# A transformer pair on one Trainium2 core: the second block's scores with the queries' lower parts in a tile of 128 rows, half of them zero

## The chip, the cores and the metric

The kernel runs on one core of one Trainium2 chip. A core has TensorE (matrix products into PSUM), VectorE, ScalarE and GpSimd (elementwise work), SyncE (issues transfers) and 16 DMA engines. The metric is device time in microseconds for one execution, the median of several.

## The reference

One sequence of 256 tokens with 2048 channels passes a first block (a mixer, memory attention, a gated feed-forward) and then a second block of two layers, which works on these tokens and on 256 context tokens. The change concerns the second block's attention. Each of its eight heads has two half heads of 64 channels, and the difference of two softmaxes is applied to the values:

```python
def _diff_attn(qb, k_all, v_all, lam):
    s = jnp.einsum('bqhid,bkhid->bhiqk', qb.astype(jnp.float32) * ATTN_SCALE, k_all.astype(jnp.float32))
    p = jax.nn.softmax(s, axis=-1)
    a = p[:, :, 0] - lam * p[:, :, 1]
    return jnp.einsum('bhqk,bkhe->bqhe', a.astype(v_all.dtype), v_all)
```

In the first layer both the tokens' and the context's queries attend (the tokens to 512 keys, the context to its own 256). In the second layer only the tokens' queries do.

## The kernel before

**Products.** An operand of 32 bits is split into an upper part of reduced precision (type fp32r) and a lower part that holds the rest, and a product is three products: upper x upper, upper x lower, lower x upper. Weights stream from memory through four buffers (raw) in pieces of 128 x 1024; ScalarE writes the upper part (whi), VectorE the lower (wlo), each into four buffers, up to three pieces ahead of TensorE (split_ahead, LK = 3). The method group runs the products of one group of weight blocks, some 96 to 192 of them, into a pair of PSUM banks (acc).

**Background work.** Everything else stands in lanes of Python generators. While group writes out the weight products, it calls tick four times per piece, and tick takes a step from each lane whose operands are ready by a planner's estimate of the engines' clocks (class Meter, costs per operation). So the order on each engine is fixed when the program is built. TensorE, VectorE, ScalarE and GpSimd each run their queue in that order.

**The scores.** qk_gen (lane q) takes the projected queries or keys of one head out of PSUM, rotates them and builds stacked tiles. For a half head i, rows 64i to 64i+63 hold its own channels. For keys, the tile st[i] has the upper part in these rows and the lower part in the other 64. For queries, st[i] has the upper part in both halves, so that one product of 128 rows gives upper x upper plus upper x lower. The queries' lower parts of both half heads lie in one tile, lo, each in its 64 rows. scores (called by attn2, lane B) then adds lower x upper with a second product, of 64 rows, into the same bank:

```python
                mm(S[i], q[i][:, o:o + P], k[i], start=True, stop=False)
                mm(S[i], ql[w, o:o + P], k[i][w], start=False, stop=True)
```

For the tokens' queries (u = 0, 1) these products have 512 columns, four per call. For the context's queries (u = 2, first layer only) they have 256 columns, eight per call. softmax2 follows on VectorE and ScalarE, attn2_t transposes the result on TensorE, and tail (lane b2) multiplies by the values and takes the head's norm, for which two small operations run on GpSimd (rstd). PSUM has four banks for all background work (aux).

**Tiles.** In the first layer the tiles st and lo come from the common heap of 60 tiles of 128 x 512 (s.qkp = s.heap in second). In the second layer they have a pool of their own, qkp, with 10 tiles (line 771).

**Lines.** Every operation goes through the planner's helper at line 342, so the trace tells operations apart by their tiles. bk is a background bank; the products of the scores show as bk<-st,st and bk<-st,lo.

Of the kernel before, what the change touches and what calls it, by code (L numbers as in the profile page):

```python
# [16 lines left out]
P = 128  # L17
# [25 lines left out]
# ---------------------------------------------------------------- the order of the weights  # L43
# [171 lines left out]
def lay(inp):  # L215
    """Layout only: every array is a reordering or a concatenation of inputs."""
# [51 lines left out]
# ---------------------------------------------------------------- when the engines get to their work  # L268
class Meter:
    """Passes instructions on and keeps an estimate of the time at which each engine is done with them, by which  # L270
    the background work is placed between the large products."""
# [24 lines left out]
    def table(s, args):  # L296
        """what it costs to get another table of functions"""
        n = next((s.TABLES[x] for x in args if isinstance(x, AF) and x in s.TABLES), s.tab)
        s.tab, old = n, s.tab
        return 0.0 if n == old else 1.28  # L300
# [45 lines left out]
# ---------------------------------------------------------------- the program  # L346
class Acc(tuple):
    """Two banks as one row of 1024"""
# [7 lines left out]
class Kern:  # L356
# [7 lines left out]
    # ---- memory  # L364
# [30 lines left out]
    # ---- background work  # L395
# [3 lines left out]
    def step(s, lane):  # L399
        """One step; a step yields the number of aux banks that it leaves in use (1 if nothing is said)"""  # L400
        q = s.lanes.get(lane)
        while q:
            s.meter.last = 0.0
            try:
                n = next(q[0])
                s.held[lane] = 1 if n is None else n
                s.ready[lane] = s.meter.last + LAG
                return True
            except StopIteration:
                q.popleft()  # L410
                s.held[lane] = 0
        return False
# [4 lines left out]
    def tick(s):  # L417
        """Steps of the background work whose operands are there by now"""
        m = s.meter.clk
        for ln in sorted(s.lanes):  # L420
            if ln != "w" and s.lanes[ln] and s.ready.get(ln, 0.0) <= m["P"] and s.fits(ln):
                s.step(ln)
        if s.lanes.get("w") and not s.quiet and m["V"] <= m["P"] + WLAG:
            s.step("w")
# [4 lines left out]
    def pump(s, lanes=None):  # L429
        """A step of the lane that is ready first; true if any did something"""  # L430
        for ln in sorted(lanes or s.lanes, key=lambda ln: (s.ready.get(ln, 0.0), ln)):
            if (lanes or ln != "w") and s.lanes[ln] and s.fits(ln) and s.step(ln) and s.meter.last:
                return True
        return False
# [8 lines left out]
    def finish_lane(s, ln, alone=False):  # L443
        """alone: the lane needs neither others nor banks"""
        s.force = alone
        while alone and s.lanes.get(ln):
            s.step(ln)
        s.force = False
        s.until(lambda: not s.lanes.get(ln))
# [4 lines left out]
    # ---- the stream of weights  # L454
# [9 lines left out]
    def split_hi(s, j):  # L464
        """The upper part of piece j"""
        q, o, w = s.subs[j]
        hi = s.hip.tile([P, MH], F32R, name=s.nm("whi"), tag="whi")
        s.nc.scalar.copy(hi[:, :w], s.raws[q][:, o:o + w])
        s.hl[j] = [hi, None]
        s.nhi = j + 1  # L470

    def split_lo(s, j):
        """What the upper part leaves"""
        q, o, w = s.subs[j]
        hi = s.hl[j][0]
        lo = s.hl[j][1] = s.lop.tile([P, MH], F32R, name=s.nm("wlo"), tag="wlo")
        s.nc.vector.tensor_sub(lo[:, :w], s.raws[q][:, o:o + w], hi[:, :w].bitcast(F32))
        s.nlo = j + 1

    def split_ahead(s, pos):  # L480
        """The parts of the pieces that come next, as far as they are there"""
        end = min(s.cur - 1 + LK, len(s.subs) - 1)
        if pos in HPOS and s.nhi <= end:
            q = s.subs[s.nhi][0]
            while s.nload < min(len(PIECES), q + EK):
                s.load_next()
            if s.there(s.raws[q]):
                s.split_hi(s.nhi)
        if pos in LPOS and s.nlo <= end and s.nlo < s.nhi:
            s.split_lo(s.nlo)  # L490
# [13 lines left out]
    def group(s, name, *segs, quiet=False, half=None):  # L504
        """The products of one group of weight blocks; segs: per 256 tokens, k -> (hi, lo). With half, the first half of
        the tokens gets ahead with the last pieces, and half(acc) is called when it is done."""
# [55 lines left out]
    # ---- small pieces  # L562
# [8 lines left out]
    def rowsum(s, parts, n):  # L571
        """[P, n] partial sums (AP) -> [P, 1]"""
        r = s.sm("rs")
        s.nc.vector.tensor_reduce(r[:, 0:1], parts, AX.X, ALU.add)
        return r[:, 0:1]

    def turned(s, get, gain, dst, ks):
        """dst[k] (hi, lo) = (x^T) * gain(k); get(t, k): [P tokens, P]"""
# [20 lines left out]
    def rb_tile(s, R, b=None):  # L599
        """R [P tokens, 2] -> [P, 256], every row the tokens' factors"""  # L600
        b = b or s.accum()
        for t in range(2):
            s.nc.tensor.matmul(b[:, t * P:t * P + P], R[:, t:t + 1].to_broadcast([P, P]), s.ident, start=True, stop=True)
        r = s.rbp.tile([P, T], F32, name=s.nm("Rb"), tag="rb")
        s.nc.scalar.copy(r, b[:, 0:T])
        return r
# [18 lines left out]
    def stats(s, x, R, xT=None):  # L625
        """the sums of squares of x[t][c] -> rstd [P, 2]; where xT is given, after it"""
# [10 lines left out]
    def stats_of(s, name, R, n=2, start=lambda: True, eng=None):  # L637
        """the same for an input"""
# [12 lines left out]
    def ahead(s, src, n=2, eng=None):  # L651
        """parts of an input, each loaded ahead of its use"""
# [8 lines left out]
    def laid(s, name):  # L661
        """an input that is laid out by columns"""
        return s.ahead([s.ap[name][i] for i in range(8)])

    def busy(s):
        """whether the DMA engines have got much to do"""
        return not s.force and s.meter.dma > s.meter.clk["P"] + DGAP

    def later(s, d):
        """nothing for d us"""  # L670
# [5 lines left out]
    def scaled(s, parts, gain, dst, gap=0.0):  # L676
        """dst[k] (hi, lo) = part k * gain(k)"""
# [18 lines left out]
    def out_chunk(s, acc, row, yg, ss, c):  # L696
        """acc [P, 2 x 512] -> yg[t] = acc * row, the sums of squares of acc into ss"""
# [8 lines left out]
    def residual(s, yg, ss, x, xn, xT, chunk, wait=True):  # L706
        """xn = x + rmsnorm(y), and what chunk(c) does with a chunk of it to get to xT"""
# [40 lines left out]
    def program(s):  # L748
# [22 lines left out]
        with s.tc.tile_pool(name="qkp", bufs=10) as s.qkp:  # L771
            s.layer(1)

    # ---------------------------------------------------------------- first block
# [110 lines left out]
    def inputs(s):  # L885
        """what the background work needs"""
# [42 lines left out]
    def shift(s, a, b):  # L929
        """z = a * R; z + (prev - z) * mu"""  # L930
# [28 lines left out]
    def rwkv(s, p):  # L959
        """Two heads; h's own rows are 64h.., its other rows hold the other side of sums over 128."""  # L960
# [124 lines left out]
        # the chunks in order  # L1085
# [212 lines left out]
    # ---------------------------------------------------------------- memory attention and the feed-forward  # L1298
    def memory_ffn(s):
# [16 lines left out]
        def normed(yg, ss, x, g, tap):  # L1316
            """x + rmsnorm(y), the next norm's transposed operand and rstd, as background work"""
# [125 lines left out]
    def ffn_up(s, acc, j, hid, Rb):  # L1443
        """blocks: gate j, value j, gate j+1, value j+1"""
# [27 lines left out]
    # ---------------------------------------------------------------- second block  # L1472
    def modulation(s, l, n0, n1):
        """columns n0..n1 (of 128) of silu(c) @ w_mod + b_mod, for c and c_ctx"""
# [64 lines left out]
        if n0 == 0:  # L1539
            # lambda  # L1540
# [10 lines left out]
    def affine(s, get, g, dst, ks):  # L1551
        """dst[k] (hi, lo) = x^T * G + B, two tiles of tokens"""
# [119 lines left out]
    def y_split(s, l):  # L1672
        """the parts of the mixed output, as they come, for the product with w_out"""
# [18 lines left out]
    def rope_half(s, a, o):  # L1692
        """a (PSUM) [P, 256] -> o rotated"""
# [8 lines left out]
    def qk_gen(s, a, parts, done, q):  # L1702
        """Rotates what is x's of a (PSUM), takes it apart, and stacks the parts of each half head: the queries' upper
        parts twice, the keys' upper and lower parts."""
# [9 lines left out]
        st, lo = [s.qkt("st"), s.qkt("st")], s.qkt("lo") if q else None  # L1714
        for i in range(2):
            A.copy(st[i][w[i]], f[w[i]])
# [3 lines left out]
            d = lo[w[i]] if q else st[i][w[1 - i]]  # L1720
# [7 lines left out]
    def attn2(s, l):  # L1728
        """the scores' softmax, head by head; attn2_t turns it"""
# [41 lines left out]
    def scores(s, l, h, u):  # L1771
# [3 lines left out]
        for i in range(2):  # L1775
            w = slice(64 * i, 64 * i + 64)
            if u < 2:
                o = qo + (T if l == 0 else 0) + u * P
                mm(S[i], q[i][:, o:o + P], k[i], start=True, stop=False)
                mm(S[i], ql[w, o:o + P], k[i][w], start=False, stop=True)  # L1780
            else:
                for t in range(2):
                    b = S[i][:, t * T:(t + 1) * T]
                    mm(b, q[i][:, t * P:(t + 1) * P], k[i][:, 0:T], start=True, stop=False)
                    mm(b, ql[w, t * P:(t + 1) * P], k[i][w, 0:T], start=False, stop=True)
# [40 lines left out]
    def tail(s, l, h, ax, ac):  # L1826
        """a head's output, its norm, transposed"""
# [32 lines left out]
    def y_tile(s, l, k):  # L1860
        """the place of part k of the mixed output"""
# [137 lines left out]
    def ln_stats(s, st, n, w):  # L1999
        """per tile of tokens: scale, bias of the normalization"""  # L2000
# [13 lines left out]
    def out1_rows(s):  # L2014
        """what the last normalization is added to"""
# [44 lines left out]
    def final(s, r, st, lg, lb, t, eng):  # L2060
        """the last normalization of a tile of tokens"""
# [27 lines left out]
```

## Time and profile before

| | us |
|---|---|
| median of 3 runs | 2938.47 (2937.62 to 2941.56) |
| span of the profiled execution | 2937.8 |
| TensorE busy in it | 2890.1 (98%) |
| VectorE busy | 2074.8 (71%) |
| ScalarE busy | 1275.3 (43%) |
| GpSimd busy | 162.4 (6%) |

The span runs from the first to the last instruction of one profiled execution. A row of a timeline or of a group names the engine, the operation, the tiles it writes and reads (out<-in), the shape, and how often. For a product, 64*128 means 64 rows by 128 columns of weights, and 64x512 the moving operand. PEld is the weight load of a product. The end of a product is modelled and products overlap, so the distance between starts tells more than a duration.

### The profile page before, as it was taken

How to read it: one execution, taken by the hardware profiler on the slowest of the kernel's cores; microseconds unless marked ns; L12 is line 12 of the kernel's file. 1: busy time of each engine (PE TensorE's matmuls, PEld its weight loads, DVE VectorE, ACT ScalarE, POOL GpSimd, SP SyncE). 2: the span in 40 equal slices, each digit the busy share in tenths (PEclk: the TensorE clock that was granted, in tenths of full speed). 3: DMA queues.
4: the chain of work that ended last, by engine and by line, in shares of the span. 5: the costliest groups of instructions: out<-in, count | busy, mean ns of one | idle time of the engine just before them, and what ended most of it. 6: DMA issues, size and time to landing. Idle time of an engine off the chain costs nothing.

```text
span 2937.8 us, 53904 instructions
## 1 busy us (share of the span) xinstructions
PE 2890.1 (98%) x22059; PEld 2692.7 (92%) x22059; DVE 2074.8 (71%) x3377; ACT 1275.3 (43%) x2110; POOL 162.4 (6%) x321
## 2 busy tenths in 40 slices
PE   8899999999999999999999999999999999999997
PEld 8788887898999899998899999999999989999996
DVE  5756755687988997988768877786344563766576
ACT  5323325555444445446443554212231463555443
POOL 1001112000000000000100000000010000000001
PEclk9899999999999999999999999999999999999998
DMA  8422335765777886777764334565243453325663
GB/s 266 135 95 92 127 95 195 274 236 172 243 237 240 306 289 225 236 250 267 256 228 166 108 115 140 202 233 195 99 133 113 160 184 101 101 87 174 200 225 134
DMA packets 150857, 538.78 MB, mean 183 GB/s; under 512 B 18240, under 2 KB 18460, under 8 KB 150608
## 3 DMA queue, kind: packets, MB, share of 16 engines
q1 hardware_dynamic: 137808, 494.92, 49.4%
q0 software_dynamic: 12656, 40.37, 4.9%
q8 instruction: 173, 2.83, 0.4%
q14 instruction: 76, 0.62, 0.1%
q10 hardware_dynamic: 144, 0.03, 0.0%
HBM read 528.66 MB, written 6.59 MB: 182 GB/s over the span
## 4 chain that ended last, share of the span: by engine, by line
PE 96%; DVE 2%; DMA 1%; ACT 1%; issue 0%; POOL 0%; SPq 0%; DVEq 0%; ACTq 0%; POOLq 0%
PE acc L342 85%; PE bk L342 11%; DMA raw<-in_w_w_in 1%; DVE wlo L342 1%; ACT whi L342 0%; DVE res L342 0%; DVE junk L342 0%; DVE y L342 0%; DVE zrk L342 0%; ACT junk L342 0%; DVE yg L342 0%; POOL pw L342 0%; POOL R L342 0%; DVE ug L342 0%; DVE zr L342 0%
## 5 line engine op out<-in xcount | busy, mean ns | idle before, releaser
L342 PE MATMUL acc<-xT,whi 128*128 128x256 f32 x8992 | 1585.3, 286 | 13.0 <-ACT whi L342 12.1
L342 PEld LDWEIGHTS acc<-xT,whi 128*128 128x128 f32 x8992 | 1344.0, 193 | 27.9 <-ACT whi L342 13.0
L342 ACT CAST whi<-raw 128x1024 fp32r<-128x1024 f32 x738 | 771.4, 1050 | 906.4 <-PE acc L342 682.8
L342 PE MATMUL acc<-xT,wlo 128*128 128x256 f32 x4496 | 1130.3, 284 | 1.4 <-DVE wlo L342 1.4
L342 DVE TENSOR_TENSOR wlo<-raw,whi 128x1024 fp32r<-128x1024 f32 x738 | 896.2, 1220 | 275.5 <-ACT whi L342 273.5
L342 PEld LDWEIGHTS acc<-xT,wlo 128*128 128x128 f32 x4496 | 801.9, 193 | 2.2 <-DVE wlo L342 2.2
L342 DVE SCALAR_TENSOR_TENSOR junk<-wm,silu 128x1024 bf16<-128x1024 f32 x352 | 421.5, 1218 | 6.0 <-DMA wm<-in_w_mod 5.5
L342 PE MATMUL acc<-whi,xT 128*128 128x256 f32 (+1 forms) x1152 | 285.7, 332 | 0.9 <-ACT xT L342 0.9
L342 PE MATMUL acc<-whi,yh 128*128 128x256 f32 (+1 forms) x768 | 224.5, 319 | 0.0
L342 PEld LDWEIGHTS acc<-whi,xT 128*128 128x128 f32 x1152 | 195.9, 191 | 21.3 <-issue 2.0
L342 PE MATMUL acc<-wlo,yh 128*128 128x256 f32 (+1 forms) x640 | 194.7, 304 | 0.0
L342 PE MATMUL acc<-wlo,xT 128*128 128x256 f32 (+1 forms) x576 | 187.4, 325 | 0.0
L342 PEld LDWEIGHTS acc<-whi,yh 128*128 128x128 f32 x768 | 146.3, 191 | 9.9
L342 PE MATMUL acc<-whi,yl 128*128 128x256 f32 x512 | 144.9, 283 | 0.0
L342 PE MATMUL acc<-wlo,hh 128*128 128x512 f32 x352 | 137.3, 390 | 0.8 <-DVE wlo L342 0.8
L342 PE MATMUL acc<-whi,hh 128*128 128x512 f32 x352 | 137.2, 390 | 0.0
L342 PE MATMUL acc<-whi,hl 128*128 128x512 f32 x352 | 137.0, 389 | 0.0
L342 PEld LDWEIGHTS acc<-wlo,yh 128*128 128x128 f32 x640 | 122.3, 191 | 5.0
L342 PEld LDWEIGHTS acc<-wlo,xT 128*128 128x128 f32 x576 | 110.2, 191 | 7.0
L342 PEld LDWEIGHTS acc<-whi,yl 128*128 128x128 f32 x512 | 98.2, 192 | 0.0
L342 DVE TENSOR_REDUCE s<-bk 128x1 f32<-128x512 f32 (+1 forms) x80 | 54.2, 688 | 45.7 <-PE bk L342 45.6
L342 PE MATMUL acc<-whi,oT 128*128 128x512 f32 x256 | 80.5, 392 | 0.6 <-DVE oT L342 0.6
(346 smaller groups left out, 2668.0 us busy)
## 6 DMA issues: line engine op xcount, KB each, us to landing
raw<-in_w_w_in SPq DMA_DIRECT2D x334, 512.0 KB, 3.6
wm<-in_w_mod SPq DMA_DIRECT2D x192, 512.0 KB, 5.0
raw<-in_w_up SPq DMA_DIRECT2D x176, 512.0 KB, 4.1
raw<-in_w_w_out SPq DMA_DIRECT2D x108, 512.0 KB, 4.5
raw<-in_w_down SPq DMA_DIRECT2D x88, 512.0 KB, 4.5
raw<-in_w_wkv SPq DMA_DIRECT2D x16, 512.0 KB, 5.2
silu<-cond POOLq DMA_DIRECT2D x12, 512.0 KB, 7.6
raw<-in_w_wq SPq DMA_DIRECT2D x8, 512.0 KB, 3.5
```

Of the source, the lines that this page charges most:

```text
L342: return f(*a, **k)
```

## The change

Each half head's queries' lower part gets a tile of its own with 128 rows. Its 64 rows hold the lower part, the other 64 are set to zero by a memset on GpSimd. The second product of each pair then takes all 128 rows of this tile and of the keys' tile; the keys' lower parts in the other rows meet zeros. One more tile per head is needed, and the second layer's pool grows from 10 to 11. Apart from this the diff only removes comments.

```diff
@@ program
-        with s.tc.tile_pool(name="qkp", bufs=10) as s.qkp:
+        with s.tc.tile_pool(name="qkp", bufs=11) as s.qkp:
             s.layer(1)
...
@@ qk_gen
         w = [slice(0, 64), slice(64, 128)]
-        st, lo = [s.qkt("st"), s.qkt("st")], s.qkt("lo") if q else None
+        st, lo = [s.qkt("st"), s.qkt("st")], [s.qkt("lo"), s.qkt("lo")] if q else None
         for i in range(2):
+            if q:
+                s.nc.gpsimd.memset(lo[i][w[1 - i]].bitcast(F32), 0.0)
             A.copy(st[i][w[i]], f[w[i]])
             if q:
                 A.copy(st[i][w[1 - i]], f[w[i]])
             yield 0
-            d = lo[w[i]] if q else st[i][w[1 - i]]
+            d = lo[i][w[i]] if q else st[i][w[1 - i]]
             V.tensor_sub(d, f[w[i]], st[i][w[i]].bitcast(F32))
             yield 0
...
@@ scores
         for i in range(2):
-            w = slice(64 * i, 64 * i + 64)
             if u < 2:
                 o = qo + (T if l == 0 else 0) + u * P
                 mm(S[i], q[i][:, o:o + P], k[i], start=True, stop=False)
-                mm(S[i], ql[w, o:o + P], k[i][w], start=False, stop=True)
+                mm(S[i], ql[i][:, o:o + P], k[i], start=False, stop=True)
             else:
                 for t in range(2):
                     b = S[i][:, t * T:(t + 1) * T]
                     mm(b, q[i][:, t * P:(t + 1) * P], k[i][:, 0:T], start=True, stop=False)
-                    mm(b, ql[w, t * P:(t + 1) * P], k[i][w, 0:T], start=False, stop=True)
+                    mm(b, ql[i][:, t * P:(t + 1) * P], k[i][:, 0:T], start=False, stop=True)
```

## Rows read from the trace of the kernel before

**Rows 1.** From the page: busy time per engine, and the chain's shares by engine.
```profile
PE 2890.1 (98%) x22059; PEld 2692.7 (92%) x22059; DVE 2074.8 (71%) x3377; ACT 1275.3 (43%) x2110; POOL 162.4 (6%) x321
...
PE 96%; DVE 2%; DMA 1%; ACT 1%; issue 0%; POOL 0%; SPq 0%; DVEq 0%; ACTq 0%; POOLq 0%
```

**Rows 2.** Windows around the scores of the two layers: busy us per engine.
```profile
core 0: us, PE busy (x) PEld busy (x) DVE busy (x) ACT busy (x) POOL busy (x), PEclk, DMA share, GB/s
1580.00:1850.00 270.00, 270.00 (x2019) 246.21 (x2018) 208.23 (x410) 132.55 (x339) 9.93 (x16) 1.00 0.35 121
2498.00:2670.00 172.00, 172.00 (x1293) 156.36 (x1292) 120.72 (x237) 93.48 (x206) 6.23 (x14) 1.00 0.29 95
```

**Rows 3.** Tile st, whole span: durations, first and last start, forms; busy slices.
```profile
L342 PE MATMUL bk<-st,lo x96: 379/492/502, 1581.9 to 2664.1; 64*128 64x512 f32 x64, 64*128 64x256 f32 x32
...
busy tenths in 40 slices 0000000000000000000003453000000000431000
```

**Rows 4.** Timeline of TensorE, from 1580.83: start, duration, operation, tiles, shape, count.
```profile
1580.83 0.64 PE L342 MATMUL acc<-xT,whi 128*128 128x256 f32 x4
1581.31 0.40 PE L342 MATMUL acc<-xT,wlo 128*128 128x256 f32 x2
1581.55 0.39 PE L342 MATMUL bk<-st,st 128*128 128x512 f32 x1
1581.87 0.49 PE L342 MATMUL bk<-st,lo 64*128 64x512 f32 x1
1582.29 0.50 PE L342 MATMUL bk<-st,st 128*128 128x512 f32 x1
1582.72 0.50 PE L342 MATMUL bk<-st,lo 64*128 64x512 f32 x1
1583.15 0.74 PE L342 MATMUL acc<-xT,whi 128*128 128x256 f32 x4
1583.73 0.40 PE L342 MATMUL acc<-xT,wlo 128*128 128x256 f32 x2
```

**Rows 5.** Timeline of TensorE, from 1590.45.
```profile
1590.45 0.39 PE L342 MATMUL bk<-st,st 128*128 128x512 f32 x1
...
1592.06 0.66 PE L342 MATMUL bk<-cons,p 128*128 128x128 f32 x4
1592.47 0.72 PE L342 MATMUL acc<-xT,whi 128*128 128x256 f32 x4
```

**Rows 6.** Timeline of TensorE, from 1599.74.
```profile
1599.74 0.28 PE L342 MATMUL bk<-st,st 128*128 128x256 f32 x1
...
1602.14 0.66 PE L342 MATMUL bk<-cons,p 128*128 128x128 f32 x4
1602.55 0.48 PE L342 MATMUL acc<-xT,whi 128*128 128x256 f32 x2
```

**Rows 7.** Timeline of TensorE in the first block's feed-forward, from 960.28.
```profile
960.28 0.39 PE L342 MATMUL acc<-whi,hh 128*128 128x512 f32 x1
...
963.00 0.39 PE L342 MATMUL acc<-whi,hh 128*128 128x512 f32 x1
```

**Rows 8.** Groups by shape, window 1580 to 1850: busy us, mean ns, idle before.
```profile
L342 PEld LDWEIGHTS acc<-xT,whi 128*128 128x128 f32 x1064 | 146.1, 191 | 1.7 <-issue 1.7
...
L342 DVE TENSOR_TENSOR wlo<-raw,whi 128x1024 fp32r<-128x1024 f32 x33 | 40.2, 1218 | 0.1
L342 ACT CAST whi<-raw 128x1024 fp32r<-128x1024 f32 x33 | 34.8, 1056 | 1.9 <-PE acc L342 1.6
```

**Rows 9.** Groups of GpSimd, whole span.
```profile
L342 POOL TENSOR_TENSOR res<-res,lb 128x512 f32<-128x512 f32 x5 | 7.9, 1594 | 4.1 <-DVE res L342 4.1
...
L342 POOL MEMSET sv<- 64x64 f32 x12 | 1.8, 146 | 0.0
...
L342 POOL TENSOR_SCALAR pw<-tl 128x4 f32<-128x4 f32 x8 | 1.6, 194 | 331.7 <-ACT sq L342 331.7
```

## The prediction

> **What bounds the kernel now.** I read the chain that ended last first. It is 96% TensorE [rows 1], and TensorE is busy for 98% of the span [rows 1]. Then I read the stretches in which the change acts. The scores' products lie between 1581.9 and 2664.1 us, in two groups, one for each layer [rows 3]. In a window around each group, TensorE is busy for every microsecond (270.00 of 270.00 and 172.00 of 172.00) at a granted clock of 1.00, which is the higher level, 2.4 GHz. VectorE has 208.23 of 270 us and 120.72 of 172 us, ScalarE about half, GpSimd next to nothing, the DMA engines a third [rows 2]. So in both stretches nothing but TensorE's own stream sets the pace, and what leaves that stream should leave the total.
>
> Busy is not the same as moving, though: a product's row runs from its start to a modelled end, and a slow handover counts as busy. The pace is read from starts. In the timeline the weight products start 0.12 us apart (four from 1580.83 to 1581.31) [rows 4]; products of 128 rows and 512 columns start 0.227 us apart where they follow one another (12 steps from 960.28 to 963.00) [rows 7]. The scores' products don't. Each product of 128 rows (st, st) is followed by one of 64 rows (st, lo), and the starts go 1581.55, 1581.87, 1582.29, 1582.72, 1583.15: four products of 512 columns in 1.60 us [rows 4] where 0.91 would do. With 256 columns it is eight in 2.40 us (1599.74 to 1602.14) [rows 6] where 0.96 would do. Every handover between 128 and 64 rows costs 0.1 to 0.2 us on top of the product.
>
> **The change, part by part.** *The lower parts' products get 128 rows.* There are 96 of them, 64 with 512 columns and 32 with 256 [rows 3]. They stand in 32 blocks of four products (two per head in the first layer, 16, and two per head in the second, 16) and 8 blocks of eight (one per head in the first layer). No operation is removed: the number of products and their columns stay, the rows they read double, and the handovers between shapes go.
>
> A block of four ahead of weight products: 1.60 us, and the next four weight products take until 1583.73, 0.58 us where four others took 0.48 [rows 4]; together 2.18. Afterwards 4 x 0.227 + 0.48 = 1.39. Saved: 0.79. The timeline has ten such blocks.
>
> A block of four ahead of other 128-row products, transposes in nearly all cases: 1590.45 to 1592.06 is 1.61, and the four transposes take 0.41 until 1592.47 [rows 5]. Their first interval too must hold some of the late handover; I take 0.05 of it, half of what the block above shows, so 2.02 becomes 0.91 + 0.36 = 1.27. Saved: 0.75 (0.70 if nothing is in it, 0.80 if 0.10). There are 22.
>
> A block of eight: 2.40 and 0.41 until 1602.55 [rows 6]; afterwards 8 x 0.12 + 0.36 = 1.32. Saved: 1.49. There are 8.
>
> Sum: 10 x 0.79 + 22 x 0.75 + 8 x 1.49 = 7.9 + 16.5 + 11.9 = 36.3 us, 24.2 of them in the first layer and 12.1 in the second.
>
> The trace of before does not have this product, lo with 128 rows behind st with 128 rows. Its bounds are 0.227 us (the plain 128-row stream [rows 7]) and the 0.32 to 0.43 that stands there now. I take 0.227: the new product has exactly the shape of its neighbours, different operands don't slow the stream of rows 7, where three kinds alternate, and two products into one bank in a row are what every weight group does.
>
> Here a rule of the Trainium skill speaks against the change. The rows first: a weight load of 128x128 lasts 191 ns [rows 8], longer than the 120 ns between starts [rows 4], so loads run beside the product before them although both use all rows. The page "TensorE: Matmul & The Clock Gate", section "Part 3: Packing small matmuls — row/col tiling", says that a weight load overlaps a product under way only when the row group differs. By that rule a 128-row lo would have to load alone, a block of four would take 4 x (0.227 + 0.191) = 1.67 us against 1.60, and nothing would be saved. The trace contradicts it in the plain stream, so it is kept as a rival with a small chance (below).
>
> *24 more zero fills on GpSimd* (two per call of qk_gen with queries: 16 in the first layer, 8 in the second), each 64 rows x 512 columns. The trace has no such fill. From below: a fill of 64x64 took 0.146 us; from above: an addition of 128x512 there took 1.594 us [rows 9]. I take some 0.5 us, nearer to the fill. GpSimd is busy for 9.93 of 270 us [rows 2], so none of it is on TensorE's path. Who waits: the subtraction that writes lo, on VectorE, and behind it in VectorE's queue the splits of the weights (wlo). The cover is the lead of these splits. One is made every 270 / 33 = 8.2 us [rows 8], and the program makes them up to three pieces ahead, so even two pieces are 16 us. If the cover were gone, 24 x 0.5 to 24 x 1.6 = 12 to 38 us would come back. I cost it at nothing.
>
> *One more tile per head.* The second layer's pool grows from 10 to 11 with it. In the first layer these tiles come from the common heap of 60, which doesn't grow. Counting tiles in the order in which the program issues, I find at most 59 in use there; with one more for each of the two heads then in flight it is 61. So once or twice an engine will wait for a tile that is about to be let go. Bounds: nothing, or a few microseconds on ScalarE, VectorE or GpSimd, under the same cover. I cost it at nothing.
>
> VectorE's work is unchanged, in less time: 208 of 246 us in the first layer, 85% where it was 77%. What is late next is still TensorE.
>
> Against the profiled execution's span: 2937.8 - 36.3 = 2901.5 us. The median of the runs shown, 2938.47, is 0.67 us above that span; with it 2902.2, so 2902.
>
> **Rivals.** *Part of the gain is given back by VectorE.* Its spare time in the first layer would be 246 - 208 = 38 us. Waits for 16 fills at 1.6 us eat 26 of it and cost nothing. If each fill also waited for its tile, 3.2 us in all, 51 us would be eaten, 13.6 too many: 2916. For it: a full heap. Against it: the lead of the splits, and fills are issued on an idle engine ahead of what needs them.
>
> *The change doesn't do what it says*: the slow handover comes from something other than the number of rows (the operands' tiles, the bank), or the weight load can't be hidden as in the rule above. Then blocks keep 1.60 to 1.67 us, and the time is 2938 to 2941, say 2940. Against it: no pair of 128-row products in the rows shows such an interval.
>
> *Slower than before.* A fill waits on GpSimd for a free tile of the heap, and behind it in GpSimd's queue stand the two operations of a head's norm that wait for ScalarE (pw<-tl, eight in the first layer, 331.7 us of GpSimd's waiting in all [rows 9]). Until these are done the tail keeps its bank, and the next scores wait for a bank on TensorE, which is in order. TensorE has not waited at all in these stretches so far. It decides from 36.3 / 8 = 4.5 us per head on; at 6 us per head for eight heads 48 us come back, 2950.
>
> **How the numbers follow.** Forecast 0.79, at 2902, its own range 2897 to 2908 (the bounds of the transposes' share, 1.1 us either way; steps of 0.227 give or take 0.01 for 128 products, 1.3 us; the runs shown lie from 0.85 below to 3.1 above their median). VectorE gives back 0.12, at 2916. No effect 0.06, at 2940. Slower 0.03, at 2950. The range 2897 to 2916 leaves out the last two and the worse half of the second. A measurement of this kernel can tell about 0.2%, 6 us, from no change: faster by more 0.91, within it 0.06, slower 0.03.
>
> **What would show it.** In the profile of the changed kernel the 96 lo products stand with 128 rows; starts in a block are 0.227 and 0.120 us apart; blocks of four take 0.91 and of eight 0.96 us; the second layer's scores begin some 24 us earlier; TensorE still has no idle time in both windows. I am wrong if the starts stay over 0.3 us apart (the row count was not the cause), if TensorE shows waits for VectorE's splits or for p, or if GpSimd's fills show waits longer than a few microseconds with a tail's norm behind them.

## The result, and the profile after

The changed kernel took 2910.18 us (median of 4 runs, 2907.45 to 2915.15); the kernel before, with it, 2939.85 (4 runs). The ratio is 0.9891, 95% interval 0.9872 to 0.9909. The profiled execution has a span of 2911.2 us, 26.6 less than before. So it is faster, by 29.7 us where the sum was 36.3. The time is inside the stated range of 2897 to 2916, but outside the forecast's own, 2897 to 2908.

The blocks of scores are where to look first. The timeline of TensorE from 1590.46, a block of four ahead of weight products, answers [rows 4]:

```profile
1590.46 0.40 PE L342 MATMUL acc<-xT,wlo 128*128 128x256 f32 x2
1590.70 0.40 PE L342 MATMUL bk<-st,st 128*128 128x512 f32 x1
1590.93 0.40 PE L342 MATMUL bk<-st,lo 128*128 128x512 f32 x1
1591.17 0.39 PE L342 MATMUL bk<-st,st 128*128 128x512 f32 x1
1591.40 0.40 PE L342 MATMUL bk<-st,lo 128*128 128x512 f32 x1
1591.63 0.63 PE L342 MATMUL acc<-xT,whi 128*128 128x256 f32 x4
1592.10 0.40 PE L342 MATMUL acc<-xT,wlo 128*128 128x256 f32 x2
```

Four products now take 0.93 us (1590.70 to 1591.63) where they took 1.60, and the weight products behind them 0.47 instead of 0.58. A block ahead of transposes, from 1598.81, answers [rows 5]:

```profile
1598.81 0.40 PE L342 MATMUL bk<-st,st 128*128 128x512 f32 x1
...
1599.74 0.60 PE L342 MATMUL bk<-cons,p 128*128 128x128 f32 x4
1600.10 0.72 PE L342 MATMUL acc<-xT,whi 128*128 128x256 f32 x4
```

0.93 and 0.36 us, where it was 1.61 and 0.41. And a block of eight, from 1607.37, answers [rows 6]:

```profile
1607.37 0.28 PE L342 MATMUL bk<-st,st 128*128 128x256 f32 x1
1607.49 0.28 PE L342 MATMUL bk<-st,lo 128*128 128x256 f32 x1
...
1608.33 0.60 PE L342 MATMUL bk<-cons,p 128*128 128x128 f32 x4
1608.68 0.72 PE L342 MATMUL acc<-xT,whi 128*128 128x256 f32 x4
```

0.96 us instead of 2.40, at 0.12 per product. The tile view of lo answers [rows 3]; the 96 products have 128 rows:

```profile
L342 PE MATMUL bk<-st,lo x96: 283/394/398, 1590.9 to 2637.7; 128*128 128x512 f32 x64, 128*128 128x256 f32 x32
```

The same view for GpSimd alone has the new fills: their durations, what ended GpSimd's idle time ahead of them (us, times), and who waited for them (nothing stands below that line). POOL is GpSimd, DVE VectorE, ACT ScalarE, PE TensorE:

```profile
L342 POOL MEMSET lo<- x24: 518/521/529, 1542.1 to 2569.1; 64x512 f32 x24
...
  DVE junk L342: 80.8, 4
  PE bk L342: 66.9, 3
  DVE st L342: 20.9, 1
who waited for it (us, times):
```

Eight fills waited, 168.6 us in all and up to 38 us each, where the prediction had an engine waiting once or twice for a few microseconds. All eight belong to the first layer, whose tiles come from the heap; in the second layer, with 11 tiles, none waited. So I take it that they waited for a tile of the full heap. The last list is empty: nobody waited for a fill. But in four cases a head's norm stood right behind a fill that had waited, which was one of the stated signs of being wrong. GpSimd's timeline:

```profile
1651.18 0.52 POOL L342 MEMSET lo<- 64x512 f32 x1 [23.68 <-PE bk L342]
1658.93 0.19 POOL L342 TENSOR_SCALAR pw<-tl 128x4 f32<-128x4 f32 x1 [7.23 <-ACT sq L342]
...
1683.10 0.52 POOL L342 MEMSET lo<- 64x512 f32 x1 [22.41 <-PE bk L342]
1689.18 0.27 POOL L342 TENSOR_SCALAR pw<-tl 128x4 f32<-128x4 f32 x1 [5.55 <-ACT sq L342]
```

After such a fill the norm's operation still waited 5.55 to 7.80 us for ScalarE, so the fill did not delay it. The windows around the scores answer [rows 2] (columns as there):

```profile
1580.00:1830.00 250.00, 250.00 (x2051) 246.82 (x2050) 210.39 (x415) 133.59 (x338) 17.33 (x30) 1.00 0.42 138
2474.00:2640.00 166.00, 166.00 (x1342) 162.60 (x1341) 121.01 (x240) 95.17 (x209) 8.33 (x18) 1.00 0.32 102
```

TensorE is still busy throughout; VectorE is at 84% and 73% where it was at 77% and 70%. So every gain should have arrived, and a comparison of starts shows where it went. From the first score of the first layer to the first of the second it was 2498.61 - 1581.55 = 917.06 us and is 2483.87 - 1590.70 = 893.17: 23.9 us gained. From there to the end it was 439.19 and is 427.33: 11.9 gained. Together 35.8. In absolute time the second layer's scores begin only 14.7 us earlier, where some 24 had been stated, because the first score comes later, at 1590.70 instead of 1581.55: 9.15 us were lost ahead of the first product that the change touches. On TensorE the instructions up to there are the same, in the same order, in both kernels.

The loss lies between 200 and 460 us, among the first block's small products: product by product, the changed kernel is 0.2 us ahead at 188 us and 9.9 behind at 463. Windows of the kernel before and then of the changed one; the last three numbers are TensorE's granted clock, the DMA share and GB/s:

```profile
200.00:260.00 60.00, 60.00 (x453) 52.11 (x453) 30.65 (x73) 18.48 (x41) 5.86 (x11) 0.91 0.24 80
350.00:380.00 30.00, 30.00 (x391) 26.42 (x389) 16.24 (x33) 5.25 (x12) 7.30 (x15) 1.00 0.34 102
430.00:460.00 30.00, 30.00 (x195) 25.02 (x194) 12.69 (x32) 8.62 (x24) 6.80 (x12) 0.89 0.24 79
```

```profile
200.00:260.00 60.00, 60.00 (x422) 50.71 (x419) 27.56 (x67) 17.04 (x40) 3.66 (x8) 0.83 0.22 71
350.00:380.00 30.00, 30.00 (x303) 26.87 (x301) 15.01 (x26) 6.67 (x16) 2.81 (x9) 0.83 0.30 88
430.00:460.00 30.00, 30.00 (x214) 25.43 (x213) 11.65 (x28) 8.22 (x21) 1.23 (x2) 0.83 0.22 71
```

The mean clock of 0.83 means that a third of such a stretch ran at the lower level, 1.2 GHz; before it was 0.89 to 1.00. Whether this is chance or belongs to the changed program is what the first runs ask.

### The profile page after: what moved, and what is told of

It reads as the page before. It is cut to its first block, busy times and chain, and to the rows that moved or that the text cites. A ratio compares the mean times of both kernels' runs of the same rounds, so it can differ in the third digit from the quotient of the medians.

```text
span 2911.2 us, 53963 instructions
## 1 busy us (share of the span) xinstructions
PE 2863.5 (98%) x22059; PEld 2697.5 (93%) x22059; DVE 2072.5 (71%) x3377; ACT 1276.8 (44%) x2110; POOL 175.1 (6%) x345
## 4 chain that ended last, share of the span: by engine, by line
PE 95%; DVE 2%; DMA 1%; ACT 1%; issue 0%; POOL 0%; SPq 0%; DVEq 0%; ACTq 0%; POOLq 0%
PE acc L342 85%; PE bk L342 10%; DMA raw<-in_w_w_in 1%; DVE wlo L342 1%; ACT whi L342 0%; DVE res L342 0%; DVE y L342 0%; DVE junk L342 0%; DVE zrk L342 0%; ACT junk L342 0%; DVE yg L342 0%; POOL pw L342 0%; POOL R L342 0%; DVE ug L342 0%; DVE zr L342 0%
## 5 line engine op out<-in xcount | busy, mean ns | idle before, releaser
L342 PE MATMUL acc<-xT,whi 128*128 128x256 f32 x8992 | 1585.7, 286 | 12.7 <-ACT whi L342 11.9
L342 PEld LDWEIGHTS acc<-wlo,hh 128*128 128x128 f32 x352 | 66.1, 188 | 14.8 <-DVE wlo L342 1.4
```

The costliest lines, as they stand in the source:

```text
L342: return f(*a, **k)
```

## The experiments

**Both kernels again.** No edit. The granted clock of every execution was read beside its time.

> The kernel before once more, unchanged, to see how far its granted clock and its time scatter. The changed kernel gained 35.8 us in the two score stretches and lost 9.2 us between 200 and 450 us, where both programs issue the same instructions. Theory (chance: the half-clock stretches among the first block's small products fall differently in each execution): the clock over the span scatters as the changed kernel's does, some 0.986 to 0.992, and the times scatter over 5 us or more. Rival (the changed program draws a lower clock there, in every execution): this kernel stays at 0.990 or above and within 2937 to 2942.

> The changed kernel once more, unchanged. Chance: over more executions its median comes to 35 us below the kernel before, about 2905, ratio 0.988. Rival (a lower clock in every execution): it stays 29 to 31 us below, ratio 0.9895, and its clock stays 0.002 to 0.004 below that of the kernel before.

> The changed kernel again, for its clock and time. Up to now the kernel before had clocks of 0.987 to 0.992 in 17 executions (2950.7 to 2937.2 us) and the changed one 0.986 to 0.990 in 8 (2915.2 to 2904.8). At the same clock of 0.989 they stood at about 2943 and 2907.5. Chance: the mean clock of both comes together with more executions, and at equal clocks the difference stays at 35 to 37 us. Rival (a lower clock of its own): the mean clock stays 0.0015 below that of the kernel before, and the difference of medians stays at some 33 us.

The first repetition of the changed kernel gave 2909.11 us (ratio 0.9876, 0.9857 to 0.9896), the second 2904.66 (0.9870, 0.9852 to 0.9889). The kernel before, repeated, gave 2943.06 (ratio 1.0002 to itself, 0.9991 to 1.0014). All executions with a clock on record, by that clock (mean us, executions):

| clock over the span | before | changed | difference |
|---|---|---|---|
| 0.986 | 2949.2 (1) | 2914.3 (2) | 34.9 |
| 0.987 | 2949.7 (9) | 2912.9 (1) | 36.8 |
| 0.988 | - | 2910.3 (1) | - |
| 0.989 | 2943.4 (13) | 2907.6 (3) | 35.8 |
| 0.990 | 2942.3 (6) | 2905.1 (4) | 37.2 |
| 0.991 | 2939.7 (9) | 2903.1 (1) | 36.6 |
| 0.992 | 2938.3 (6) | - | - |
| median of all | 2943.0 (44) | 2907.45 (12) | 35.6 |

Both kernels scatter over 12 to 14 us, and the clock tells nearly all of it. At equal clocks they stand 35 to 37 us apart, which is the sum of the blocks. The last four executions of the changed kernel had 0.990, 0.990, 0.991 and 0.990, so a low clock does not belong to it; its profile then has, from 200 to 260 us, what the kernel before had:

```profile
200.00:260.00 60.00, 60.00 (x451) 52.16 (x452) 30.74 (x73) 18.47 (x41) 5.86 (x11) 0.91 0.25 80
```

The rival falls. A small difference of the mean clock, 0.9888 in 12 executions against 0.9895 in 44, is too small to tell from this scatter. The three runs from which the forecast started lay at the fast end: 2938.47 us where the median of 44 is 2943.0.

**Fewer handovers, same products.** The kernel before, its products reordered within each block: all of 128 rows first, then all of 64 rows.

```diff
-        for i in range(2):
-            w = slice(64 * i, 64 * i + 64)
-            if u < 2:
-                o = qo + (T if l == 0 else 0) + u * P
+        w = [slice(0, 64), slice(64, 128)]
+        if u < 2:
+            o = qo + (T if l == 0 else 0) + u * P
+            for i in range(2):
                 mm(S[i], q[i][:, o:o + P], k[i], start=True, stop=False)
-                mm(S[i], ql[w, o:o + P], k[i][w], start=False, stop=True)
+            for i in range(2):
+                mm(S[i], ql[w[i], o:o + P], k[i][w[i]], start=False, stop=True)
...
```

> The kernel before, with one edit: the products of 64 rows stay, but in each block all products of 128 rows come first and all of 64 rows after them, so there is one handover to 64 rows and one back instead of two of each (in a block of eight: instead of four of each). Theory (the handovers cost, 0.1 us into 64 rows and 0.2 us out of them): blocks of four take 0.227 + 0.322 + 0.227 + 0.43 = 1.21 us instead of 1.61, blocks of eight 6 x 0.12 + 0.21 + 0.31 = 1.24 instead of 2.40; 22 us gained, 2918. If products on the two halves of the rows also run beside each other, blocks of four take 0.98 and the gain is some 31 us. Rival (a product of 64 rows is slow by itself, or the pause hangs on the operands): blocks keep about 1.6 and 2.4 us, 2940.

It took 2913.5 us (ratio 0.9895, 0.9879 to 0.9912); at a clock of 0.989 its mean is 2913.0, 30.4 below the kernel before. The timeline of a block:

```profile
1581.33 0.63 PE L342 MATMUL bk<-st,st 128*128 128x512 f32 x2
1581.89 0.50 PE L342 MATMUL bk<-st,lo 64*128 64x512 f32 x2
1582.33 0.74 PE L342 MATMUL acc<-xT,whi 128*128 128x256 f32 x4
```

Four products take 1.00 us. The two of 64 rows start 3 ns apart, and the next product starts 0.44 us after them, where it started 0.42 to 0.43 after one alone [rows 4]: the two take the time of one. One handover into them (0.33 from the start of the second product of 128 rows to them, where 0.23 is the plain interval) and one out of them (the 0.44) remain. So a product of 64 rows is not slow; the changes of shape are, and their number decides. The gain is the one that was stated for products that run beside each other.

**The same with one half of the rows.** The grouped kernel, but both products of 64 rows read rows 0 to 63. It leaves out the second half head's own lower part, so only its time is of use.

```diff
-                mm(S[i], ql[w[i], o:o + P], k[i][w[i]], start=False, stop=True)
+                mm(S[i], ql[w[0], o:o + P], k[i][w[0]], start=False, stop=True)
...
-                    mm(S[i][:, t * T:(t + 1) * T], ql[w[i], t * P:(t + 1) * P], k[i][w[i], 0:T],
+                    mm(S[i][:, t * T:(t + 1) * T], ql[w[0], t * P:(t + 1) * P], k[i][w[0], 0:T],
```

> As the kernel with grouped products (128 rows first, then 64), but both half heads' products of 64 rows read rows 0 to 63, so the second half head's scores get the wrong lower part; shapes and number of products are the same. In the grouped kernel the two products of 64 rows started 3 ns apart. Theory (they run beside each other because they stand on different halves of the rows): here they start 0.21 to 0.23 us apart (512 columns), as two queries of one head do in the first block's attention; blocks of four take 1.21 us. Rival (two short products overlap whatever rows they use): again 3 ns apart and 0.99 us.

```profile
1580.18 0.63 PE L342 MATMUL bk<-st,st 128*128 128x512 f32 x2
1580.74 0.73 PE L342 MATMUL bk<-st,lo 64*128 64x512 f32 x2
1581.40 0.74 PE L342 MATMUL acc<-xT,whi 128*128 128x256 f32 x4
```

The block takes 1.22 us: on the same rows the two products go one after the other. Their starts are 0.34 us apart, where 0.21 to 0.23 was expected, and the way out is then 0.32 rather than 0.44; the sum is as stated. Here nothing runs beside anything, and one handover each way costs 1.22 - 0.93 = 0.29 us over the changed kernel's block, where two cost 1.60 - 0.93 = 0.67. One execution took 2916.33 us at a clock of 0.991, 23.4 below the kernel before at that clock; 22 had been stated, with the grouped kernel, for one handover each way without products beside each other.

**One part alone.** The changed kernel with the blocks of eight back at 64 rows.

```diff
-                    mm(b, ql[i][:, t * P:(t + 1) * P], k[i][:, 0:T], start=False, stop=True)
+                    mm(b, ql[i][64 * i:64 * i + 64, t * P:(t + 1) * P], k[i][64 * i:64 * i + 64, 0:T], start=False, stop=True)
```

> The changed kernel, but the context's queries' blocks of eight go back to products of 64 rows (of the new tiles); the blocks of four keep 128 rows. Theory (each block's handovers cost what they cost, independent of the rest): blocks of four 0.93 us, blocks of eight 2.40; 12 us of the gain go, 24 us remain: some 12 us above the changed kernel, 2916 to 2922. Rival (the gain comes from the timing of the background work as a whole, not from the blocks): nothing like 12 us of difference to the changed kernel.

It took 2916.54 us (ratio 0.9912, 0.9895 to 0.9929). At a clock of 0.990 it stands at 2916.5, 11.4 above the changed kernel and 25.8 below the one before; a block of eight takes 2.40 us again (1597.18 to 1599.58). The blocks' gains add up one by one.

**The price of the fills.** Each fill eight times, then 24 times; the extra ones are hidden from the planner, so that the other engines' order stays.

```diff
                 s.nc.gpsimd.memset(lo[i][w[1 - i]].bitcast(F32), 0.0)
+                for _ in range(7):
+                    s.nc._nc.gpsimd.memset(lo[i][w[1 - i]].bitcast(F32), 0.0)
```

> The changed kernel with each zero fill written eight times instead of once (7 more fills that the planner does not see, so the order on the other engines stays): 8 x 0.52 = 4.2 us per half head on GpSimd instead of 0.52, and 24 x 7 x 0.52 = 87 us more of GpSimd's work. Theory (the fill lies under the lead of the weights' splits, 12 us and more, and some microseconds ahead of what needs it): no change, within 3 us of the changed kernel. Rival (the fills are on the path or disturb VectorE): up to 80 us more.

> The same with 24 fills for each: 12.5 us per half head, 25 us per head. Fills of the changed kernel start some 5 us ahead of the subtraction that needs them, so VectorE would wait some 7 us for the first half head and as much again for the second, beyond the 12 us by which the wlo splits lead. Theory (the cover is that lead, and it ends): TensorE waits, some 2 to 10 us per head, 20 to 100 us in all. Rival (GpSimd's fills never reach TensorE): no change.

Eightfold fills gave 2906.11 us (ratio 0.9886, 0.9864 to 0.9908), within the scatter of the changed kernel; at a clock of 0.990 its three executions have 2903.6 to 2906.1, the changed kernel 2903.5 to 2906.3. GpSimd is then busy for 65.28 of 250 us and TensorE still for all 250.00. The fills cost nothing at 4.2 us per half head either. The room behind them was nearly used up, though: the norm that had waited 5.55 us for ScalarE now waits 1.61.

```profile
1679.94 0.27 POOL L342 TENSOR_SCALAR pw<-tl 128x4 f32<-128x4 f32 x1 [1.61 <-ACT sq L342]
```

With 24 fills it was 2940.03 us (ratio 0.9990, 0.9977 to 1.0003): the whole gain gone. But not the way that I had stated. TensorE's waits from 1580 to 1830 us (total, times, longest):

```profile
PE bk L342 <- DVE sq L342: 16.0, 4, 4.5
PE bk L342 <- POOL lo L1719: 4.6, 2, 3.4
```

No wait is for a weight split, and no subtraction on VectorE waited for a fill. The smaller one is TensorE's own wait for a fill. The larger one is for a head's norm. The timeline of such a place:

```profile
1668.54 0.19 POOL L342 TENSOR_SCALAR pw<-tl 128x4 f32<-128x4 f32 x1
1668.81 1.01 POOL L342 TENSOR_TENSOR tl<-pw,mhalf 128x4 f32<-128x4 f32 x1
...
1669.85 0.69 DVE L342 TENSOR_TENSOR sq<-bk,tl 128x512 f32<-128x512 f32 x1 [7.19 <-POOL tl L342]
...
1670.69 0.66 PE L342 MATMUL bk<-cons,sq 128*128 128x128 f32 x2 [4.50 <-DVE sq L342]
```

In GpSimd's queue the norm's two operations stood behind the fills and ran without a pause after them; VectorE waited 7.19 us for them and TensorE 4.50 for VectorE. That is the mechanism of the rival on the slower side, with 24 fills in front of the norm in place of a wait for a tile. The waits add up to 20.6 us in this layer. The rest is the clock: from 1669 to 1676 us, at the end of that wait and after it, it was 0.52 on average, and from 1580 to 1830 us it was 0.97 where the changed kernel had 1.00. By an estimate from these two numbers that is 0.03 x 250 = 7.5 us. Together with the waits it makes 28.1 of the 28.5 us by which the span of this profiled execution (2939.7) exceeds that of the changed kernel (2911.2); both had a clock of 0.83 in the three windows between 200 and 460 us. The executions have 0.982 to 0.987.

## Why the prediction was right, point by point

**What bounds the kernel.** TensorE's own stream, as read: in both windows it stays busy throughout, and removing time from it removed that time from the span.

**The blocks.** The intervals are 0.93 us per block of four where 0.91 was taken (0.232 each instead of 0.227, 0.7 us over 32 blocks) and 0.96 per block of eight as stated. The first interval of the transposes did hold 0.05 us of the last handover: it went from 0.41 to 0.36. So 36.3 becomes 35.8 measured, 23.9 and 11.9 by layer where 24.2 and 12.1 were stated.

**The cause.** That the pause belongs to the change between 128 and 64 rows was inferred from the starts. The grouped kernel, with one handover each way per block instead of two or four, and the one-half kernel show it: with the same products, the time falls with the number of handovers.

**The rule against the change.** The Trainium skill, page "TensorE: Matmul & The Clock Gate", section "Part 3: Packing small matmuls — row/col tiling", lists weight loads as overlapping products under way only where the row group differs. The runs contradict that line for the plain 128-row stream: intervals of 0.120 us stand beside loads of 192 ns (the groups by shape of the changed kernel). An earlier sentence of the same section, which the prediction left out, also lets a load into the background weight buffer run ahead; the stream fits it, but no run shows which buffer a load goes to.

What changes at a handover is seen in the rows of the weight loads (PEld). In the kernel before, the load for the product of 64 rows that starts at 1581.87:

```profile
1581.87 0.18 PEld L342 LDWEIGHTS bk<-st,lo 64*128 64x128 f32 x1 [0.25 <-issue]
```

In the changed kernel, the load for the product that starts at 1590.93:

```profile
1590.70 0.19 PEld L342 LDWEIGHTS bk<-st,lo 128*128 128x128 f32 x1
```

Between these products of 128 rows the load begins 0.23 us ahead of its own product; at a change of shape the two begin together. The Trainium skill, page "TensorEngine Tiling (Array Packing)", section "Key Properties", says that a change of tiling mode drains the engine. The trace agrees so far, and gives the price that the page doesn't: some 0.3 us for a change to 64 rows and back. By the starts of the kernel before that is 0.1 in and 0.2 out, but in the one-half kernel a part of it falls between the two products of 64 rows. Whether the time goes into draining or into a load that may not run ahead, no run here separates.

**The fills and the heap.** 0.521 us each, where 0.5 was taken. The waits for tiles were sized wrong, eight of up to 38 us instead of one or two of a few, but nobody waited for GpSimd. So the cost of nothing was right, and for another reason than the one given: the cover that I named first, the lead of the weight splits, was not the one that held or gave way. The norms behind the fills, which stood in the slower rival, had 5.55 us to spare, 1.61 with eightfold fills and nothing with 24. The prediction had no number for this margin.

**The level.** Here a step was off. I set the sum against 2938.47, the median of three runs, as if the level were known to a microsecond, and took the scatter of these runs, 0.85 below to 3.1 above, for that of the kernel. The 2938.47 stands 4.5 us below the median of 44 executions, which reach from 2937.2 to 2951.0. The changed kernel's median over 12 is 2907.45, that is 5.4 above 2902: 4.5 from the level and 0.5 from the sum (the rest is scatter). The first median, 2910.18, is nearer to the 2916 of the rival with VectorE than to the forecast; that it was not this rival is read from the windows, in which TensorE waits for nothing. In the first comparison 6 us of the gain were hidden: 2.7 because the changed kernel's four executions, two of them at 0.986 and 0.987, stood above its median of 12, and 3.2 because those of the kernel before stood below its median of 44. In the profiled execution the clock hid 9.

## What to carry to other kernels

Read TensorE's pace from starts, not from busy time: a stretch that shows no idle time at all lost 36 us to changes between 128-row and 64-row products. Where a short product stands alone among full ones, pad it with zeros to full rows, or put short ones on different halves of the rows next to each other, so that there are few changes of shape. If the zeros come from another engine, look at what stands behind the fills in that engine's queue, and how long it can wait: that gave way at 24 fills, with GpSimd busy for 184 of 250 us. And before a difference of 0.2% is explained, look at the granted clock of each execution: compare at equal clocks.

## What the runs showed of the hardware that I had not expected

- Two products of 64 rows on different halves of the rows start 3 ns apart and take together the time of one (0.44 us to the next product, against 0.42 to 0.43), in the middle of a stream of 128-row products; on the same half they start 0.34 us apart.
- With TensorE busy for 60.00 of 60 us, the granted clock still was 0.83 in one execution and 0.91 in another, among the first block's small products (64*64, 128*64 and others). Busy time in a profile does not say which clock is granted.
- In the kernel with 24 fills the clock fell to the lower level towards the end of a wait of 4.50 us and stayed there after TensorE went on at 1670.69 (0.50 from 1671 to 1676 us), so that the wait cost more than itself.
- At a change between 128 and 64 rows the weight load does not begin ahead of its product, while between the changed kernel's products of 128 rows it begins 0.23 us ahead, though both use all rows.
